# Layer 1's last six gate and up pairs by seven quarter products instead of eight, with B's plain blocks ahead of them and one set of down weights for both halves

## The chip, the cores and the metric

The kernel runs on one core of one Trainium2 chip. The metric is device time in microseconds (us); less is better. TensorE (PE in the profile) does the matmuls, VectorE (DVE), ScalarE (ACT) and GpSimd (POOL) do the rest, and SyncE (SP) and ScalarE issue most DMAs.

## The reference

Two layers over x of 1024 positions by 1024 features, fp32, each with a mixer and a SwiGLU feed-forward of 2816 hidden features. Layer 0's mixer is a gated MLP beside trailing means; layer 1's is RWKV-7, a recurrence over positions whose output `y * g` is multiplied by `w_o`.

```python
def swiglu(hn, w_gate, w_up, w_down):
    return (jax.nn.silu(hn @ w_gate) * (hn @ w_up)) @ w_down

for layer in range(DEPTH):
    hn = rms_norm(h, mix_norm[layer])
    h = h + mixer(hn)            # layer 0: gMLP and pooling; layer 1: RWKV-7, (y * g) @ w_o
    h = h + swiglu(rms_norm(h, ffn_norm[layer]), ffn_w_gate[layer], ffn_w_up[layer], ffn_w_down[layer])
return rms_norm(h, final_norm)
```

## The kernel before

**Tiling.** The positions are two halves, A and B, of 512 each (`HT`). Features stand on the partitions in eight chunks of 128, so a half of an activation is eight tiles of 128x512. The hidden features are 22 blocks of 128, in 11 pairs. A fp32 product is made of three matmuls on rounded parts: high by high, high weight by low activation, low weight by high activation (`mm3`, L408; `split`, L158, makes the parts: ScalarE copies the high part, VectorE subtracts it, L160, for the low one). One gate or up block for one half is therefore 8 chunks by 3 = 24 matmuls of 128x512; a down block for one half is 24 as well.

**Seven products.** In layer 0, pairs 4 to 10 (`PORDER`) are made by a scheme of the Strassen and Winograd kind. A unit is one pair's gate or up weights (1024 by 256) against both halves. Its four weight quarters and four activation quarters are combined by additions, and seven quarter products (`quarter`, L739, 12 matmuls each) give what eight would. `full_steps` (L790) does it: `weights` (L794) makes the weight sums on VectorE (L797 to L806) and splits them; the activation sums t1 to t4 were made earlier. `first_steps` (L759) makes half A's plain block of a unit from two quarter products, and can keep the first of them, p1, in DRAM (`p1_d`) for `full_steps`, which then does five (60 matmuls). Layer 1 is plain everywhere before the change: `ffn` (L947) goes through groups of blocks, gates, ups and then their down products, for one half at a time.

**Order of the weights.** `plan` is a list of all weight loads in the order of their use. `take` (L147) hands out the next entry, starts the loads of the following ones and their splitting; all loads are issued from ScalarE's queue (L123) into three slots named `raw`. Entries can be pieces of an activation too: `push_act(("y", 1), ...)` puts the four pieces of the recurrence's output y, which goes through DRAM (`y_d`), into the same plan and the same three slots.

**Layer 1's end, before.** `recur` (L1474) runs half B's recurrence while `drive` (L1042) feeds it dense work of half A: `dense_a`, `ffn` over `TAIL`. When the recurrence's output of the last step (`yp`, L1496) is there, `post` normalizes it per head (L1698 to L1723), TensorE transposes it (`sm<-ident,ysb`), VectorE gates it (`gch`, L1740) and SyncE stores it (L1743). Half A's remaining gate, up and down blocks go on meanwhile, and y's pieces are loaded and split between them. `out_b` then does `out_proj` (L1783) for half B, B's norm follows, half A ends with `final_down` (L1798, the last down products in transposed form with the final norm), and half B's whole feed-forward ends the kernel, with its own loads of all gate, up and down weights. `residual` (L506) adds a finished product to the stream on VectorE (L507). In the profile dense products are L409 to L411, quarter products L744 to L746, final ones L1810 to L1812.

Of the kernel before, what the change touches and what calls it, by code (L numbers as in the profile page):

```python
# [9 lines left out]
F32 = mybir.dt.float32  # L10
F32R = mybir.dt.float32r
AF = mybir.ActivationFunctionType
ALU = mybir.AluOpType
# [28 lines left out]
PORDER = (4, 5, 6, 7, 8, 9, 10)  # L42


@with_exitstack
def tile_trunk(
# [175 lines left out]

    def push_ffn_event(l, h, kind, f, lean=False):
# [71 lines left out]
    p1_d = dram.tile([P, 2 * PAIRS, HT], F32, name="p1_d")  # L295
# [59 lines left out]
    y1, o1, begun = push_act(("y", 1), y_d[1]), push_o(1), False  # L355
    TAIL = G1A[1] + G1A[2] + G1A[3]
    for e in ffn_events(TAIL, True):
        begun = begun or e == ("u", G1A[2][0][0])
        if e == ("u", G1A[3][0][0]):
            for go in o1:  # L360
                go()
        if e[0] != "d":
            push_ffn_event(1, 0, *e)
        if begun and e[0] in "gu":
            next(y1, None)
    push_ffn(1, 1)
# [387 lines left out]
    def save_hidden(fp, h, f, s):  # L754
        t = fp.tile([P, 2, HT], F32R, tag="hid", bufs=2, name="hid")
        split(s, t[:, 0, :], t[:, 1, :])
        sp.dma_start(hid_d[h][:, f], t.bitcast(F32))

    def first_steps(blocks, hn, fp):  # L759

        b11, b21 = (parts_of(hn, slice(k, k + 4)) for k in (0, 4))
        sg, prev = {}, []

        def second(i, f, n, w, o):
            quarter(o, parts_of(w, HI), b21, False)
            if n == 0:
                sg[f] = fp.tile([P, HT], F32, tag="t2", bufs=2, name="sg")
                act.activation(sg[f], o, AF.Silu)
            else:
                s = sg.pop(f)  # L770
                dve.tensor_tensor(out=s, in0=s, in1=o, op=ALU.mult)
                save_hidden(fp, 0, f, s)

        for i, f, n, kept in blocks:
            w = take(("first", f, n))
            o = mmt()
            quarter(o, parts_of(w, LO), b11, True)
            if kept:
                t = fp.tile([P, HT], F32, tag="t1", bufs=2, name="p1")
                act.activation(t, o, AF.Copy)  # L780
                sp.dma_start(p1_d[:, 2 * i + n, :], t)
            yield 0.5
            if prev:
                second(*prev.pop())
                yield 0.5
            prev.append((i, f, n, w, o))
        second(*prev.pop())
        yield 0.5

    def full_steps(blocks, kept, x, fp, wp):  # L790
# [3 lines left out]
        def weights(i):  # L794
# [12 lines left out]
            c = [wp.tile([P, D], F32R, tag=t, bufs=2, name=t) for t in ("chi", "clo")]  # L807
# [11 lines left out]
        makes["full0"], makes["full1"] = weights0, weights  # L819
# [5 lines left out]
        def finish(i, n, j, s, psum=None):  # L825
# [4 lines left out]
            else:  # L830
                dve.tensor_tensor(out=s, in0=gates.pop((i, j)), in1=s if psum is None else psum, op=ALU.mult)
                save_hidden(fp, j % 2, 2 * i + j // 2, s)

        for i, n in blocks:
            k = i in kept
            a = mmt()
            w = take(("full0", i, n))
# [10 lines left out]
            b, c, d = take(("full1", i, n))  # L848
# [98 lines left out]
    def ffn(l, h, hn, fp, groups=GROUPS, last=False, nd=3, after=None, between=iter(()), early=False, then={}):  # L947
# [3 lines left out]
        for kind, f in ffn_events(groups, early):  # L951
            if kind in "gu" and last and f in groups[-1] and len(turned) < 4 and (kind, f) != ("g", groups[-1][0]):
# [26 lines left out]
            else:  # L979
# [6 lines left out]
                for m in range(KT):  # L986
# [7 lines left out]
                    if m == KT - 1 and f[-1] in then:  # L994
                        then[f[-1]]()
# [36 lines left out]
    def exhaust(gen):  # L1032
        for _ in gen:
            pass
# [753 lines left out]
    def turn(h, j):  # L1788

        t = fin_pool.tile([P, D], F32, tag="turn", bufs=4, name="turn")  # L1790
# [284 lines left out]
    flag, hnB = [], []  # L2075

    def out_b():
        exhaust(out_proj(1, ys))
        hnB.extend(norm_split(1, C_FFN + 8, b))

    def y_pieces():
        while not flag:
            yield
        yield from take_act(("y", 1))

    dense_a = ffn(
        1, 0, hnA, f, TAIL, last=True, between=y_pieces(), early=True,
        then={G1A[1][-1][-1]: lambda: flag.append(1), G1A[2][0][-1]: out_b},
    )
    drive(until(dense_a, flag), recur(1, wp, in_pieces(hp, 0, h_d[0, 1]), RATIO), RATIO)  # L2090
    wp_es.close()
    ps_es.close()
    ps_es = open_psum("psd2", DENSE)
    b, b_es = open_pool(name="act3", bufs=1, side="left")
    hb_pool, hb_es = open_pool(name="hb2", bufs=1, side="left")
    fin_pool, fin_es = open_pool(name="fin", bufs=1, side="left")
    fgb = fin_pool.tile([P, D], F32, name="fgb")
    act.dma_start(fgb, final_norm.partition_broadcast(P))
    reload(hb_pool, 1, h_d[1, 1])
    ys = open_act(("y", 1), b)  # L2100
    drive(dense_a)
    drive(ffn(1, 1, hnB, f, last=True, early=True))
    for e in (fin_es, hb_es, b_es, hp_es, nxt["a_es"], f_es, ps_es):
        e.close()
# [30 lines left out]
```

## Time and profile before

| what | value |
|---|---|
| median of 3 runs (lowest, highest) | 2382.71 us (2379.66, 2390.3) |
| the profiled execution's own time | 2386.18 us |
| its span | 2384.4 us |
| mean granted TensorE clock | 0.987 |
| PE busy | 2315.2 us, 97% |
| DVE busy | 1465.3 us, 61% |
| ACT busy | 947.4 us, 40% |
| DMA | 347.97 MB, mean 146 GB/s |

The profile describes one execution. Its first part gives each engine's busy time and share, its second the span in 40 slices, its fourth the chain of work that ended last. A row of the timeline reads: start in us, duration, engine, line, operation, output<-inputs, and in brackets how long the engine had been idle and what it waited for. A row of the table of windows gives, for a stretch of time, each engine's busy time with the number of its instructions, then the granted TensorE clock, the DMA engines' busy share and GB/s.

### The profile page before, as it was taken

What the parts mean: (1) busy time and instruction counts of PE and PEld (TensorE: products, weight loads), DVE (VectorE), ACT (ScalarE), POOL (GpSimd) and SP (SyncE); (2) the same over time, 40 slices, a digit from 0 to 9 for tenths busy, and PEclk for the clock granted to TensorE, in tenths of its full rate; (3) what the DMA queues carried; (4) which work ended last, traced back from release to release, by engine and by line L of the source; (5) the groups of instructions that cost most, each with busy time, mean ns of one, the idle gap of its engine ahead of it and who ended that gap; (6) DMA issues with size and microseconds to landing.
All of it is one profiled execution on the core that took longest, in us unless ns stands there. A gap on an engine that the chain in (4) does not pass through costs nothing.

```text
span 2384.4 us, 37572 instructions
## 1 busy us (share of the span) xinstructions
PE 2315.2 (97%) x15315; PEld 1892.5 (79%) x15315; DVE 1465.3 (61%) x2312; ACT 947.4 (40%) x1467; POOL 182.5 (8%) x207
## 2 busy tenths in 40 slices
PE   8999999999999999999989899999999999999998
PEld 6888888888888888777767678787778788888886
DVE  6445775656567958757768858856664546443443
ACT  6233443444223765423336565433232225222223
POOL 0200000000000022101100122201010001000001
PEclk9999999999999999999989999999999999999999
DMA  5114473333765476776545475776525324333231
GB/s 182 53 45 143 150 193 97 107 111 128 290 234 193 144 191 157 220 220 171 145 138 139 143 197 148 210 221 181 158 85 162 116 80 133 115 97 97 83 112 45
DMA packets 422605, 347.97 MB, mean 146 GB/s; under 512 B 95200, under 2 KB 368736, under 8 KB 420128
## 3 DMA queue, kind: packets, MB, share of 16 engines
q10 hardware_dynamic: 266048, 195.33, 27.7%
q1 hardware_dynamic: 155168, 146.05, 20.0%
q0 software_dynamic: 1216, 4.20, 0.8%
q8 instruction: 120, 1.97, 0.4%
q14 instruction: 53, 0.43, 0.1%
HBM read 266.47 MB, written 79.04 MB: 145 GB/s over the span
## 4 chain that ended last, share of the span: by engine, by line
PE 83%; DVE 7%; DMA 4%; ACT 2%; issue 2%; POOL 1%; SPq 0%; ACTq 0%; POOLq 0%; DVEq 0%
PE mm L409 19%; PE mm L411 19%; PE mm L410 19%; PE mm L744 5%; PE mm L746 5%; PE mm L745 5%; PE sm L1496 4%; DVE wlo L160 1%; DMA raw<-y_d 1%; DVE it L1448 1%; PE yp L1496 1%; PE aux L1420 1%; PE aux L1421 1%; PE mm L594 1%; PE aux L1422 1%
## 5 line engine op out<-in xcount | busy, mean ns | idle before, releaser
L409 PE MATMUL mm<-ahi,whi 128*128 128x512 f32 x1376 | 542.5, 397 | 12.8 <-ACT ahi L159 11.9
L411 PE MATMUL mm<-ahi,wlo 128*128 128x512 f32 x1376 | 542.1, 394 | 3.7 <-DVE wlo L160 3.7
L410 PE MATMUL mm<-alo,whi 128*128 128x512 f32 x1376 | 542.6, 394 | 2.3 <-DVE alo L160 2.3
L159 ACT ACTIVATE whi<-raw 128x1024 fp32r<-128x1024 f32 (+2 forms) x284 | 286.4, 1014 | 522.6 <-PE mm L410 410.6
L160 DVE TENSOR_TENSOR wlo<-raw,whi 128x1024 fp32r<-128x1024 f32 (+2 forms) x284 | 340.4, 1202 | 223.6 <-ACT whi L159 206.1
L409 PEld LDWEIGHTS mm<-ahi,whi 128*128 128x128 f32 x1376 | 260.0, 189 | 71.6 <-ACT ahi L159 13.2
L411 PEld LDWEIGHTS mm<-ahi,wlo 128*128 128x128 f32 x1376 | 260.0, 189 | 60.6 <-DVE wlo L160 4.6
L410 PEld LDWEIGHTS mm<-alo,whi 128*128 128x128 f32 x1376 | 260.2, 189 | 59.8 <-DVE alo L160 4.0
L507 DVE TENSOR_TENSOR h<-h,mm 128x512 f32<-128x512 f32 x276 | 186.3, 685 | 161.7 <-PE mm L411 157.2
L969 DVE TENSOR_TENSOR sg<-sg,mm 128x512 f32<-128x512 f32 x52 | 35.7, 687 | 138.3 <-PE mm L411 138.3
L409 PE MATMUL mm<-hidhi,wdhi 128*128 128x512 f32 x304 | 117.9, 394 | 1.9 <-ACT sg L961 1.9
L410 PE MATMUL mm<-hidlo,wdhi 128*128 128x512 f32 x304 | 119.6, 394 | 0.0
L411 PE MATMUL mm<-hidhi,wdlo 128*128 128x512 f32 x304 | 119.5, 393 | 0.0
L744 PE MATMUL mm<-ahi,whi 128*128 128x512 f32 x296 | 115.7, 391 | 0.0
L745 PE MATMUL mm<-alo,whi 128*128 128x512 f32 x296 | 115.3, 390 | 0.0
L746 PE MATMUL mm<-ahi,wlo 128*128 128x512 f32 x296 | 113.7, 390 | 0.0
L159 ACT ACTIVATE wdhi<-raw 128x1024 fp32r<-128x1024 f32 x42 | 43.4, 1057 | 161.9 <-PE mm L410 117.8
L409 PEld LDWEIGHTS mm<-hidhi,wdhi 128*128 128x128 f32 x304 | 57.5, 189 | 14.6 <-ACT sg L961 2.3
L160 DVE TENSOR_TENSOR wdlo<-raw,wdhi 128x1024 fp32r<-128x1024 f32 x42 | 51.4, 1224 | 27.7 <-ACT wdhi L159 27.7
L411 PEld LDWEIGHTS mm<-hidhi,wdlo 128*128 128x128 f32 x304 | 57.5, 189 | 12.3 <-issue 0.5
L410 PEld LDWEIGHTS mm<-hidlo,wdhi 128*128 128x128 f32 x304 | 57.4, 189 | 11.9
L744 PEld LDWEIGHTS mm<-ahi,whi 128*128 128x128 f32 x296 | 55.6, 188 | 11.7 <-issue 0.2
(394 smaller groups left out, 4232.9 us busy)
## 6 DMA issues: line engine op xcount, KB each, us to landing
raw<-in_ffn_w_down_dram ACTq DMA_DIRECT2D x88, 512.0 KB
raw<-in_ffn_w_gate_dram ACTq DMA_DIRECT2D x74, 512.0 KB
raw<-in_ffn_w_up_dram ACTq DMA_DIRECT2D x74, 512.0 KB
hid_d<-hid SPq DMA_DIRECT2D x36, 512.0 KB
ar<-ab_d SPq DMA_DIRECT2D x16, 1024.0 KB
hd<-hid_d SPq DMA_DIRECT2D x26, 512.0 KB
raw<-in_ab_w_in_dram ACTq DMA_DIRECT2D x16, 512.0 KB
raw<-in_ab_w_out_dram ACTq DMA_DIRECT2D x16, 512.0 KB
```

The costliest lines, as they stand in the source:

```text
L159: act.activation(hi, src, AF.Copy)
L160: (eng or dve).tensor_tensor(out=lo, in0=src, in1=hi.bitcast(F32), op=ALU.subtract)
L409: pe.matmul(o, whi, xhi, start=first, stop=False)
L410: pe.matmul(o, whi, xlo, start=False, stop=False)
L411: newest[0] = pe.matmul(o, wlo, xhi, start=False, stop=last).ins
L507: dve.tensor_tensor(out=H[h][:, m, :], in0=H[h][:, m, :], in1=o, op=ALU.add)
L594: pe.matmul(ops[j], xhi[:, k, sl], whi[:, kk], start=(k == 0), stop=False)
L744: pe.matmul(o, wh[:, k, :], x[0][:, k, :], start=st, stop=False, skip_group_check=True)
L745: pe.matmul(o, wh[:, k, :], x[1][:, k, :], start=False, stop=False, skip_group_check=True)
L746: pe.matmul(o, wl[:, k, :], x[0][:, k, :], start=False, stop=k == 3, skip_group_check=True)
L969: dve.tensor_tensor(out=s, in0=s, in1=o, op=ALU.mult)
L1496: i = f(*args, **kw)
```

## The change

Pairs 5 to 10 of layer 1 (`LATER`), 12 units, are made by seven products. The new order is:

- `dense_a` beside the recurrence covers only blocks 2 to 9 of half A with their downs, and its `then` hook, now called ahead of the last down group, makes the first two units' plain block of half A (`first_steps` with `keep`, key `first1`, p1 and hidden rows to DRAM). H[0] is stored to `hs_d`.
- After the recurrence come four more such units, between them the loads of y's four pieces; then `out_proj` for B, then the last six units, beside which B's norm is made (`norm_b`).
- `plain_b` makes B's blocks 0 to 9 plainly (480 matmuls); beside it `combine1` makes the activation sums t1 to t4 from rows that it loads from `nb_d` and `n_d[1]`.
- `full_steps` over the 12 units, five quarter products each (720 matmuls). The tile `c` (the split of two weight sums) uses the buffers of `b12` (`pair_of`).
- `last_downs`: for blocks 10 to 19 both halves with one set of weights, then blocks 0 to 9 for B, then blocks 20 and 21 by `final_down`, A then B. Hidden rows come from `hid1_d`.

```diff
+LATER = (5, 6, 7, 8, 9, 10)
+AHEAD_IN = 2
...
-    TAIL = G1A[1] + G1A[2] + G1A[3]
+    UNITS = mats(LATER)
+    TAIL = groups_to(2, 2 * LATER[0])
+    GD = [[2 * i, 2 * i + 1] for i in LATER[:-1] + tuple(range(LATER[0])) + LATER[-1:]]
...
     for e in ffn_events(TAIL, True):
+        if e == ("d", TAIL[-1]):
+            push_units(UNITS[:AHEAD_IN])
...
-    push_ffn(1, 1)
+    y1 = push_act(("y", 1), y_d[1])
+    push_units(UNITS[AHEAD_IN : AHEAD_IN + 3])
+    for unit in (UNITS[AHEAD_IN + 3], None, None):
+        next(y1)
+        if unit:
+            push_units([unit])
+    next(y1)
+    for go in push_o(1):
+        go()
+    push_units(UNITS[AHEAD_IN + 4 :])
...
-    drive(until(dense_a, flag), recur(1, wp, in_pieces(hp, 0, h_d[0, 1]), RATIO), RATIO)
+    drive(dense_a, recur(1, wp, in_pieces(hp, 0, h_d[0, 1]), RATIO), RATIO)
...
+    reload(hb_pool, 1, h_d[1, 1])
+    ys = open_act(("y", 1), xa)
+    got_y = take_act(("y", 1))
...
+    exhaust(first_steps(all_units[AHEAD_IN : AHEAD_IN + 4], hnA, f, "first1", hid1_d, between=y_calls()))
+    exhaust(got_y)
...
+    exhaust(out_proj(1, ys, after_b))
...
+    drive(first_steps(all_units[AHEAD_IN + 4 :], hnA, f, "first1", hid1_d), norm_b(norm_bcast(acc[0])), 2.0)
...
+    drive(plain_b(), combine1(), 1.0)
...
+    cs = [b.tile([P, 4, HT], F32R, tag="b12" + t, name="c" + t) for t in ("hi", "lo")]
...
+    steps = full_steps(UNITS, LATER, x, f, wp, "Full", hid1_d, pair_of)
...
-    drive(ffn(1, 1, hnB, f, last=True, early=True))
+    exhaust(last_downs())
```

**What moves.** Everything up to the middle of half B's recurrence stands as before, with line numbers 33 to 46 higher. The next rows are TensorE's at the recurrence's end; `sm<-ident,ysb` are the eight transposes of y, `hidhi` and `wdlo` belong to half A's down products, `ahi` and `whi` to gate and up products. Before:

```order
L411 MATMUL mm<-ahi,wlo 128x512
L409 MATMUL mm<-ahi,whi 128x512
L1496 MATMUL sm<-ident,ysb 128x128 x7
L410 MATMUL mm<-alo,whi 128x512
L411 MATMUL mm<-ahi,wlo 128x512
```

And in the change:

```order
L444 MATMUL mm<-hidhi,wdlo 128x512
L1540 MATMUL sm<-ident,ysb 128x128 x8
L777 MATMUL mm<-ahi,whi 128x512
L778 MATMUL mm<-alo,whi 128x512
L779 MATMUL mm<-ahi,wlo 128x512
```

Before, 78 matmuls of 128x512 stand between the last `yp` product and the seven transposes (68 ahead of the first of the eight); now 30, all of them down products. Behind the transposes stand 34 quarter-product matmuls of units 2 to 4, then second quarters of these.

The next rows are ScalarE's queue at the same place; `raw<-y_d` is the load of a piece of y into a weight slot, `ahi` its split, `sg`, `t` and `hidhi` belong to blocks of half A. Before:

```order
L159 ACTIVATE wdhi<-raw 128x1024
L123 DMA raw<-y_d_83 128x1024
L159 ACTIVATE ahi<-raw 128x1024
L159 ACTIVATE whi<-raw 128x1024
L972 ACTIVATE hidhi<-sg 128x512
L123 DMA raw<-in_ffn_w_down_dram 128x1024
```

And in the change, from the recurrence's last copy on:

```order
L1690 ACTIVATE ysb<-yp 128x512
L1759 ACTIVATE ysb<-ysb,mean,var 128x64 x8
L125 DMA raw<-y_d_82 128x1024
L125 DMA raw<-in_ffn_w_up_dram 128x8x128
L125 DMA raw<-y_d_82 128x1024
L822 ACTIVATE t_16825<-mm 128x512
L161 ACTIVATE ahi<-raw 128x1024
L822 ACTIVATE t_16847<-mm 128x512
L125 DMA raw<-y_d_82 128x1024
L161 ACTIVATE ahi<-raw 128x1024 x2
L125 DMA raw<-y_d_82 128x1024
L161 ACTIVATE whi<-raw 128x1024
```

Before, weight loads, splits and hidden rows of half A stood between y's pieces. Now the first piece's load follows the last `ysb` work directly, and the next weights (`whi`) and the copies of p1 (`t`) stand behind it.

SyncE's queue there, where `y_d<-gch` is y's store, `p_d` the store of a p1, `hid_d_89` hidden rows of the new scheme, `hs_d_91` half A's stream and `h<-h_d` the 2 MB reload of half B's stream. Before:

```order
L1743 DMA y_d_83<-gch 1024x1x128
L1684 DMA gch<-g_d_1981 128x8x128
L1743 DMA y_d_83<-gch 1024x1x128
L1845 DMA h<-h_d_87 128x4096
```

And in the change:

```order
L1728 DMA gch<-g_d_1986 128x8x128
L812 DMA hid_d_89<-hidhi 128x512
L812 DMA hid_d_89<-hidlo 128x512
L2121 DMA hs_d_91<-h 128x512 x7
L1889 DMA h<-h_d_86 128x4096
L2121 DMA hs_d_91<-h 128x512
L1787 DMA y_d_82<-gch 1024x1x128
L823 DMA p_d<-t_16825 128x512
```

The last store of y stood ahead of the reload of half B's stream and now stands behind it and behind the stores of half A's stream.

More of the change, by code (lines that the diff above doesn't have):

```diff
@@ L771, in second @@
                 dve.tensor_tensor(out=s, in0=s, in1=o, op=ALU.mult)
-                save_hidden(fp, 0, f, s)
+                if lean:
+                    ts = [fp.tile([P, HT], F32R, tag=t, bufs=3, name=t) for t in ("hidhi", "hidlo")]
+                    split(s, *ts)
+                    for j in range(2):
+                        sp.dma_start(to[0][:, f, j], ts[j].bitcast(F32))
+                else:
+                    save_hidden(fp, 0, f, s, to)
         for i, f, n, kept in blocks:
-            w = take(("first", f, n))
+            w = take((key, f if key == "first" else i, n))
             o = mmt()
@@ L785, in first_steps @@
                 yield 0.5
+            next(between, None)
             prev.append((i, f, n, w, o))
@@ L2074, in tile_trunk @@
     hnA = nxt["hn"]
[L2075 to L2084, printed above, removed]
+    all_units = [(i, 2 * i, n, True) for i, n in UNITS]
     dense_a = ffn(
-        1, 0, hnA, f, TAIL, last=True, between=y_pieces(), early=True,
-        then={G1A[1][-1][-1]: lambda: flag.append(1), G1A[2][0][-1]: out_b},
-    )
-    drive(until(dense_a, flag), recur(1, wp, in_pieces(hp, 0, h_d[0, 1]), RATIO), RATIO)
@@ new lines, in tile_trunk, with after_b, norm_b @@
+    exhaust(got_y)
+    acc, add = running_sums(1)
+    def after_b(m):
+        sp.dma_start(hs_d[1][:, m, :], H[1][:, m, :])
+        add(m)
+    exhaust(out_proj(1, ys, after_b))
+    x = {n: [b.tile([P, 4, HT], F32R, tag=n + t, name=n + t) for t in ("hi", "lo")] for n in ("b12", "b22")}
+    def norm_b(bc_):
+        for m in range(KT):
+            t = nt.tile([P, HT], F32, tag="nsq", bufs=2, name="hn")
+            dve.scalar_tensor_tensor(
+                out=t, in0=H[1][:, m, :], scalar=col(C_FFN + 8 + m), in1=bc_, op0=ALU.mult, op1=ALU.mult
+            )
+            split(t, *(y[:, m % 4, :] for y in x["b12" if m < 4 else "b22"]))
+            sp.dma_start(nb_d[:, m, :], t)
+            yield 1.0
@@ new lines, in plain_b @@
+    def plain_b():
+        for fd in range(2 * LATER[0]):
+            for kind in "gu":
+                w = take((kind, 1, 1, fd))
+                o = mmt()
+                quarter(o, parts_of(w, LO), x["b12"], True)
+                yield 0.5
+                quarter(o, parts_of(w, HI), x["b22"], False)
+                if kind == "g":
+                    s = f.tile([P, HT], F32, tag="t2", bufs=2, name="sg")
+                    act.activation(s, o, AF.Silu)
+                else:
+                    dve.tensor_tensor(out=s, in0=s, in1=o, op=ALU.mult)
+                    save_hidden(f, 1, fd, s, hid1_d)
+                yield 0.5
@@ new lines, in last_downs @@
+    def last_downs():
+        turned, wd = {0: [], 1: []}, {}
+        for gi, g in enumerate(GD):
+            for fd in g:
+                wd[fd] = take(("D", fd))
+            if gi + 1 < len(GD):
+                load_hid(gi + 1, hslot)
+            if gi + 1 == len(GD):
+                break
+            for h in halves_of(gi):
+                for m in range(KT):
+                    o = mmt()
+                    ms = slice(m * P, (m + 1) * P)
+                    for i, fd in enumerate(g):
+                        hd = held[h, fd]
+                        mm3(o, wd[fd][0][:, ms], wd[fd][1][:, ms], hd[:, 0, :], hd[:, 1, :], i == 0, i == 1)
+                    residual(m, h, o)
+                    if gi == len(GD) - 2 and m % 2:
+                        turned[0].append(turn(0, m // 2))
+        for h in range(2):
+            hid = {fd: (held[h, fd][:, 0, :], held[h, fd][:, 1, :]) for fd in g}
+            if h == 0:
+                turned[1].extend(turn(1, j) for j in range(4))
+            yield from final_down(h, g, wd, hid, turned[h])
```

142 lines of the change are left out of this document (114 added, 28 removed).

## The prediction

> **What bounds the kernel now.** I read the page first: which engine fills the span, and the chain that ended last.
>
> ```profile
> PE 2315.2 (97%) x15315; PEld 1892.5 (79%) x15315; DVE 1465.3 (61%) x2312; ACT 947.4 (40%) x1467; POOL 182.5 (8%) x207
> ```
>
> ```profile
> PE 83%; DVE 7%; DMA 4%; ACT 2%; issue 2%; POOL 1%; SPq 0%; ACTq 0%; POOLq 0%; DVEq 0%
> ```
>
> TensorE is busy 97% and 83% of the chain. Matmuls left out are worth their full time only where nothing else becomes late, so I read the stages next, in the table of windows.
>
> ```profile
> 200.00:600.00 400.00, 400.00 (x1770) 330.84 (x1769) 253.59 (x366) 165.92 (x257) 2.56 (x3) 1.00 0.44 134
> 600.00:700.00 100.00, 99.09 (x435) 81.16 (x435) 57.38 (x75) 22.63 (x25) 5.11 (x5) 1.00 0.72 257
> 1230.00:1265.00 35.00, 22.12 (x72) 16.81 (x71) 26.60 (x42) 16.33 (x24) 1.20 (x2) 0.71 0.81 241
> 1800.00:1900.00 100.00, 98.15 (x432) 80.73 (x431) 45.80 (x53) 26.83 (x32) 0.00 (x0) 1.00 0.41 124
> 2100.00:2300.00 200.00, 200.00 (x884) 165.71 (x883) 83.49 (x95) 50.93 (x62) 0.00 (x0) 1.00 0.32 97
> ```
>
> 200 to 600 is layer 0's own stage of seven products, 600 to 700 its down products from stored hidden rows, 1230 to 1265 the place where half A's y of layer 1 comes back from DRAM, 1800 on the stage that the change rewrites. There TensorE has almost nothing to gain in waits; the waits from 1600 on say the same:
>
> ```profile
> PE sm L1496 <- DVE gt L1537: 4.5, 3, 2.8
> PE mm L409 <- ACT sg L961: 1.9, 1, 1.9
> ```
>
> The 4.5 us lie inside the recurrence, which stays. The 1.9 us are the one wait of the dense stage (98.15 of 100 between 1800 and 1900); its code goes.
>
> **Fewer products.** A unit plainly costs 2 blocks x 2 halves x 24 = 96 matmuls; by seven products 84. Twelve units: 144 fewer. At full rate 400 us / 1770 = 0.226 us each, so 144 x 0.226 = **-32.5 us**, all of it on the path, and -1.9 us with the wait above.
>
> **The turn of y: the dearest term.** Rows of the recurrence's end, in the timeline:
>
> ```profile
> 1768.80 0.92 PE L1496 MATMUL yp<-uv,gt 128*64 128x64 f32 x24
> ...
> 1782.42 0.68 DVE L1723 TENSOR_TENSOR ysb<-ysb,vch 128x512 f32<-128x512 f32 x1
> ...
> 1787.63 0.93 PE L1496 MATMUL sm<-ident,ysb 128*128 128x128 f32 x7
> 1788.16 2.16 DVE L1740 SCALAR_TENSOR_TENSOR gch<-sm,vec,gch 128x128 f32<-128x128 f32 x8 [0.29 <-PE sm L1496]
> ```
>
> Call the end of the last yp product, 1769.7, T0. y is ready for the transposes at 1783.1, T0+13.4, by VectorE's and ScalarE's normalization. Before, 68 matmuls (15.4 us) covered that; now 30 (6.8 us). VectorE has about two fewer residual additions between (of the size of the 0.68 us row, 0.5 to 0.7 each, so about -1.0), so TensorE idles from about +6.8 to +12.4: **5.6 us**. What comes then is seen once already, in layer 0's end, where half A's y goes through DRAM with little to cover it:
>
> ```profile
> 1231.76 0.54 SPq L1743 DMA_DIRECT2D y_d<-gch  x1
> 1235.35 1.49 ACTq L123 DMA_DIRECT2D raw<-y_d  x3
> 1240.70 2.23 ACT L159 ACTIVATE ahi<-raw 128x1024 fp32r<-128x1024 f32 x2 [2.67 <-DMA raw<-y_d]
> ...
> 1241.81 0.79 PE L409 MATMUL mm<-ahi,whi 128*128 128x512 f32 x1 [8.89 <-ACT ahi L159]
> ...
> 1244.22 2.61 ACTq L123 DMA_DIRECT2D raw<-in_rwkv_w_o_dram  x4
> ...
> 1244.54 0.63 PE L411 MATMUL mm<-ahi,wlo 128*128 128x512 f32 x1
> ...
> 1248.38 0.63 PE L411 MATMUL mm<-ahi,wlo 128*128 128x512 f32 x1
> ...
> 1250.05 1.06 ACT L159 ACTIVATE whi<-raw 128x1024 fp32r<-128x1024 f32 x1 [1.81 <-DMA raw<-in_rwkv_w_o_dram]
> ```
>
> From store to load 3.59 us, from load to split 5.35, from a w_o load to its split 5.83. After the idle 8.89 us the matmuls between 1244.54 and 1248.38 start (1248.38 - 1244.54) / 9 = 0.427 us apart instead of 0.226, nearly half speed, and ten of them lose 2.0 us. The window's 72 records, of 155 that fit 35 us at full rate, say that this place loses up to 18.7 us in all.
>
> The Trainium skill, "TensorE: Matmul & The Clock Gate", Part 1, speaks against new gaps: a gate passes half of the clock's pulses after an idle window of about 3.4 us and opens after about as long busy. The trace agrees on the factor (0.427 to 0.226). As an estimate from the page a gap costs 3.4 x 1/2 = 1.7 us, and the sum below, with two long gaps, would be 2 x 0.3 = 0.6 us lower by it.
>
> The walk with these durations: transposes 1.2 and gch 2.2 us bring the store to +16, the first load of y to +19.5, its split to +25. TensorE meanwhile has 34 matmuls from +13.6, ten at half clock: 7.7 + 2.0, to +23.3. Then come second quarters, which need copies of p1 that stand behind y's load in ScalarE's queue: the first is there at +21, the second stands behind the split of the first piece, +26: **1 us**. At +29.3 the next unit's weights are wanted (`whi` at the end of the ScalarE rows). Their split stands behind that of the third piece of y, whose slot comes free with the low part of the first (+27.3), lands +5.35 later and is split in 1.1: +33.7, so **4.4 us**. `out_proj`'s first weights wait for a slot in the same ring and 5.83 us more: about **2.7 us**, and the second quarter beside it **1.4** for its copy of p1 (both estimates of the same walk). With half clock after the two longest gaps, 2.0 each: 5.6 + 2.0 + 1 + 4.4 + 2.0 + 2.7 + 1.4 = **+19 us**. Bounds: 8 us (the transposes and their half clock alone; the rest hidden by the matmuls behind) and 25 us (5.6 and the 18.7 that layer 0's place loses). I take 19, near layer 0's figure, since the queue is the same. SyncE's queue is the reason why the store could be later still: the 2 MB reload and eight stores of half A's stream stand ahead. An issue takes about 0.5 us, as the store's own row has it, and doesn't wait for its landing; they go out while y is still normalized, so nothing is added.
>
> **B's norm.** Its chain in layer 0 runs from the sums to the first product:
>
> ```profile
> 1244.14 0.16 DVE L454 TENSOR_SCALAR nrs<-aux 128x4 f32<-128x4 f32 x1
> ...
> 1251.37 0.75 DVE L1111 SCALAR_TENSOR_TENSOR hn<-h,vec,aux 128x512 f32<-128x512 f32 x1 [1.88 <-PE aux L461]
> ```
>
> 7.2 us and eight scaled rows behind it. Six units, 144 matmuls or 32.5 us, cover that; without them it would cost 7 to 15. I take +0.5 (0 to 3). `combine1` puts 16 subtractions and 16 low parts beside 480 matmuls: nothing (cover 108 us against some 22 of VectorE).
>
> **The stage of five products.** 12 units of 60 matmuls, 13.55 us each. VectorE has 17 operations of 128x512 per unit (four sums, five low parts of weights, three copies with p1, two additions, 1.5 gating products and 1.5 low parts of hidden rows). In layer 0:
>
> ```profile
> 345.00:600.00 255.00, 255.00 (x1126) 211.25 (x1126) 152.68 (x227) 107.25 (x176) 0.00 (x0) 1.00 0.35 117
> ```
>
> ```profile
> DVE s3lo L160 <- ACT s3hi L159: 22.3, 12, 5.3
> DVE hid L160 <- ACT hid L159: 11.2, 17, 0.7
> DVE wlo L160 <- ACT whi L159: 10.0, 9, 3.1
> DVE s L797 <- DMA raw<-in_ffn_w_up_dram: 6.1, 7, 1.2
> ```
>
> ```profile
> L160 DVE TENSOR_TENSOR wlo<-raw,whi 128x512 fp32r<-128x512 f32 x28 | 18.9, 687 | 2.3 <-ACT whi L159 1.7
> L159 ACT ACTIVATE whi<-raw 128x512 fp32r<-128x512 f32 x28 | 16.8, 628 | 6.4 <-PE mm L745 3.9 <-DVE raw L800 1.7 <-PE mm L746 0.8
> ```
>
> A unit there takes 84 x 0.226 = 19.0 us of TensorE (so 13.4 units in 255 us) and 152.68 / 13.4 = 11.4 us of VectorE, with TensorE never waiting. Now it is 17 x 0.687 = 11.7 against 13.55, or 86%: it fits, but closely. `s3hi` has a single buffer, so ScalarE splits (0.628) only after TensorE's last use in the unit before, and TensorE then wants it: some 0.7 us in every second unit, **+4 us** (0 to 12). At the stage's start the tile `c` must wait for the last use of `b12` before the second raw slot empties and the next load comes: **+1.7** (0 to 4; a load and its split are 5.4 to 5.8 us, of which a product or two hide most).
>
> **The last downs.** For B's groups alone two blocks' weights and hidden rows, 2 MB, go with 48 matmuls, 10.8 us: 194 GB/s. The row 600 to 700 has 257 GB/s with TensorE at 99.09%. About 1% of 100 us: **+1** (0 to 4), the order of the two final parts included. The new 136 issues on SyncE wait for nothing that TensorE needs but the ones above.
>
> **The sum.** 2386.2 - 32.5 - 1.9 + 19 + 0.5 + 4 + 1.7 + 1 = 2378.0 against the profiled execution's 2386.18. That lies 3.5 above the median of the runs, so in terms of the median **2374.5**. A measurement of this kernel tells about 0.5% (12 us: below 2370.8, above 2394.6) from no change.
>
> **Rivals.**
> 1. *y is covered after all.* The 24 second-quarter matmuls and the products of units 4 and 5 hide the loads, and only the transposes' wait and its half clock remain (8 us instead of 19), and `s3hi` never makes TensorE wait (0 instead of 4), as in layer 0, whose row 200 to 600 has no wait with the same single buffer. For it: before, y went through DRAM beside dense work and cost 1.9 us. Against: three raw slots for y, w_o and weights together. Time: 2374.5 - 11 - 4 = 2359.5. Faster.
> 2. *VectorE becomes the bound of the five-product stage.* If the waits for ScalarE and loads in layer 0's rows are not slack but stay with each unit, they add (22.3 + 11.2 + 10.0 + 6.1) / 13.4 = 3.7 us to 11.7: 15.4 us a unit against 13.55, so 12 x 1.85 = 22 us in place of 4. Time 2374.5 + 18 = 2392.5; with the turn at its upper bound (+6) 2398.5. It decides from 13.55 us a unit on. Against: `s3lo`'s wait is longest 5.3 us, which looks like VectorE running ahead of TensorE. Centre 2396, slower.
> 3. *The saving isn't there:* matmuls were not the limit. The rows at 400.00 of 400 and 200.00 of 200 exclude it; under 0.02.
>
> **How the numbers follow.** The forecast with its own range of 2365 to 2384 has 0.46, rival 1 0.32, rival 2 0.17, the rest 0.05. Faster by over 0.5% needs under 2370.8: rival 1 nearly whole (0.30) and a quarter of the forecast's case (0.11): 0.41. Slower, above 2394.6: most of rival 2 and some of the rest, 0.14. Within: 0.45. The range takes rival 1 with its good half, down to 2352, and rival 2 up to 2397.
>
> **What would show it.** In the profile after: 144 fewer 128x512 matmuls; TensorE idle before the transposes of y by 5 to 6 us and half clock behind; a wait on `whi` of 4 us some 20 us later, none if rival 1 holds; waits on `s3hi` in the five-product stage, with VectorE under 90% there; over 95% and TensorE waiting for VectorE's `wlo` or `clo` in every unit is rival 2. A wait on the raw loads of hidden rows in the last 110 us would be a term I left out, and a recurrence that itself runs longer would make the reading of the order wrong.

## The result and the profile after

| | before | changed |
|---|---|---|
| median of 7 runs each | 2386.00 us (2379.66 to 2395.07) | 2368.74 us (2367.38 to 2372.49) |
| ratio, 95% interval | | 0.9924 [0.9908, 0.994] |
| profiled execution, its span | 2386.18, 2384.4 us | 2372.49, 2370.8 us |

The change is faster by 0.76%, 17 to 18 us. The forecast was 8 us less than the kernel before (2374.5 against the 2382.71 of three runs; those three lay low). The direction held, and the gain is twice what was forecast as likeliest. The measured time lies in the range, 2352 to 2397, but that range is wide enough to hold a gain of 31 us and a loss of 14.

The windows of the kernel after, with the same columns as those of before:

```profile
200.00:600.00 400.00, 400.00 (x1770) 330.74 (x1770) 252.87 (x365) 166.03 (x258) 2.56 (x3) 1.00 0.44 134
...
1760.00:1850.00 90.00, 80.60 (x423) 65.05 (x418) 44.70 (x72) 28.81 (x42) 2.90 (x1) 0.94 0.64 200
...
2040.00:2203.00 163.00, 159.42 (x697) 130.33 (x697) 119.02 (x183) 49.27 (x77) 0.00 (x0) 1.00 0.55 188
2260.00:2360.00 100.00, 100.00 (x474) 82.89 (x472) 61.50 (x89) 30.86 (x58) 10.82 (x12) 1.00 0.33 116
```

1760 to 1850 is the turn of y, with 9.4 us of TensorE idle; the five-product stage lasts from 2003 to 2168, so 2040 to 2203 holds most of it and 35 us of down products. VectorE is at 73% there, and also in the stage alone (119.5 of 164 us), not at the 86% of the prediction: 189 operations stand in those 164 us instead of 204, in part because the first two units' weight sums are made earlier; and operations of 687 ns start as little as 600 ns apart, so their busy times overlap. The downs from 2260 on have no wait. TensorE's waits from 1600 us on:

```profile
PE sm L1540 <- DVE ysb L1767: 6.2, 4, 3.7
PE mm L777 <- ACT whi L161: 5.2, 2, 4.2
PE mm L777 <- ACT s3hi L161: 3.0, 6, 0.5
PE sm L1540 <- DVE gt L1581: 1.9, 2, 1.1
PE mm L777 <- DVE t L905: 1.1, 1, 1.1
```

**The turn of y went mostly as walked.** From its timelines (T0, the end of the last yp product, is 1765.7 here):

```profile
1764.53 1.15 PE L1540 MATMUL yp<-uv,gt 128*64 128x64 f32 x32
...
1776.44 0.45 PE L1540 MATMUL sm<-ident,ysb 128*128 128x128 f32 x1 [3.74 <-DVE ysb L1767]
1777.97 1.73 PE L1540 MATMUL sm<-ident,ysb 128*128 128x128 f32 x7 [1.08 <-DVE ysb L1767]
...
1781.07 0.54 SPq L1787 DMA_DIRECT2D y_d<-gch  x1
...
1785.98 0.34 ACTq L125 DMA_DIRECT2D raw<-y_d  x1
...
1798.97 0.50 PE L777 MATMUL mm<-ahi,whi 128*128 128x512 f32 x1 [4.19 <-ACT whi L161]
```

TensorE idles 4.8 us before the transposes, in two parts (3.74 and 1.08; 5.6 forecast), the store goes out at T0+15.4 (+16), the first load of y at +20.3 (+19.5), and TensorE waits 4.2 us for the weights behind y's third piece (4.4), up to +33.3 (+33.7). `out_proj`'s first weights and the copy of p1 beside them cost nothing (2.7 and 1.4 forecast). Behind both gaps the clock is half:

```profile
1778.00:1782.00 4.00, 4.00 (x13) 3.47 (x14) 2.16 (x8) 0.00 (x0) 0.00 (x0) 0.50 0.63 260
1782.00:1786.00 4.00, 4.00 (x17) 3.27 (x16) 0.00 (x0) 0.00 (x0) 0.00 (x0) 0.91 0.47 135
...
1799.00:1803.00 4.00, 3.76 (x9) 2.75 (x10) 1.97 (x3) 1.91 (x4) 0.00 (x0) 0.60 0.58 205
```

About seven matmuls start 0.427 us apart behind each gap, so a gap costs 1.4 to 1.6 us there, not 2.0: the 1.7 us estimated from the Trainium skill, "TensorE: Matmul & The Clock Gate", Part 1, was the nearer one.

**Where the rest came from.** The start varies from execution to execution. y is transposed in sets of eight, one set for each chunk of 128 positions. The third set from the end ends a stretch of the same code in all kernels here, and in the fourteen profiles it starts between 1695.8 and 1702.0: at 1695.96 before and at 1699.89 after. Counted from them, the two profiles differ by (2384.4 - 1695.96) - (2370.8 - 1699.89) = 688.4 - 670.9 = 17.5 us, as the runs do. It divides at the last yp product:

- **Behind it 614.7 us before, 605.1 after.** At 0.2257 us each the 2612 and 2478 matmuls take 589.5 and 559.3, so 25.2 and 45.8 us are something else: +20.6 us, where the prediction had 19 + 0.5 + 4 + 1.7 + 1 - 1.9 = +24.3.
- **Ahead of it 73.8 us before, 65.8 after.** Ten matmuls (2.3 us) moved behind it. The other 5.7 us are nowhere in the prediction.

The timelines show a place for the 5.7 us. Before:

```profile
1714.45 1.06 ACT L159 ACTIVATE wdhi<-raw 128x1024 fp32r<-128x1024 f32 x1 [4.37 <-DMA raw<-in_ffn_w_down_dram]
...
1715.54 1.23 DVE L160 TENSOR_TENSOR wdlo<-raw,wdhi 128x1024 fp32r<-128x1024 f32 x1 [3.90 <-ACT wdhi L159]
1716.68 1.28 DVE L1537 TENSOR_TENSOR gt<-sm,gm 128x512 f32<-128x512 f32 x2
...
1717.42 1.98 PE L1496 MATMUL sm<-ar 64*64 64x128 f32 x30 [2.77 <-DVE gt L1537]
```

And in the change at the same step of the recurrence:

```profile
1717.52 1.29 DVE L1581 TENSOR_TENSOR gt<-sm,gm 128x512 f32<-128x512 f32 x2 [2.08 <-PE sm L1540]
```

Before, VectorE stood at the low part of block 10's down weight, for whose load ScalarE had waited 4.37 us, with the recurrence's gt behind it; TensorE idled 2.77 us, and half clock followed, here in the windows before (the change's clock is 1.00 there):

```profile
1719.00:1723.00 4.00, 4.00 (x71) 3.56 (x66) 2.67 (x4) 0.00 (x0) 0.00 (x0) 0.50 0.95 250
```

In the change the last group of half A's blocks there is 8 and 9, there is no third down weight at that place, and gt waits for TensorE instead.

### The profile page after: what moved, and what is told of

It is laid out like the page before. It is cut to its first block, busy times and chain, and to the rows that moved or that the text cites. A ratio compares the mean times of both kernels' runs of the same rounds, so it can differ in the third digit from the quotient of the medians.

```text
span 2370.8 us, 37920 instructions
## 1 busy us (share of the span) xinstructions
PE 2283.6 (96%) x15171; PEld 1861.3 (79%) x15171; DVE 1552.3 (65%) x2496; ACT 952.7 (40%) x1507; POOL 181.8 (8%) x207
## 5 line engine op out<-in xcount | busy, mean ns | idle before, releaser
L162 DVE TENSOR_TENSOR wlo<-raw,whi 128x1024 fp32r<-128x1024 f32 (+2 forms) x274 | 314.1, 1151 | 164.8 <-ACT whi L161 135.8
L443 PE MATMUL mm<-alo,whi 128*128 128x512 f32 x864 | 342.2, 396 | 2.4 <-DVE alo L162 2.1
L442 PE MATMUL mm<-ahi,whi 128*128 128x512 f32 x832 | 329.4, 399 | 13.1 <-ACT ahi L161 11.5
L444 PE MATMUL mm<-ahi,wlo 128*128 128x512 f32 x832 | 328.7, 395 | 2.9 <-DVE wlo L162 2.9
L777 PE MATMUL mm<-ahi,whi 128*128 128x512 f32 x488 | 193.0, 396 | 5.6 <-ACT whi L161 5.2
L442 PEld LDWEIGHTS mm<-ahi,whi 128*128 128x128 f32 x832 | 157.1, 189 | 50.7 <-ACT ahi L161 12.8
L778 PE MATMUL mm<-alo,whi 128*128 128x512 f32 x488 | 191.1, 392 | 0.0
L779 PE MATMUL mm<-ahi,wlo 128*128 128x512 f32 x488 | 188.7, 391 | 0.0
L442 PE MATMUL mm<-hd,dhi 128*128 128x512 f32 x368 | 144.4, 392 | 1.1 <-DVE h L540 1.1
L444 PE MATMUL mm<-hd,dlo 128*128 128x512 f32 x368 | 143.4, 390 | 0.0
L443 PE MATMUL mm<-hd,dhi 128*128 128x512 f32 x368 | 143.2, 389 | 0.0
L777 PEld LDWEIGHTS mm<-ahi,whi 128*128 128x128 f32 x488 | 92.4, 189 | 26.8 <-ACT whi L161 6.1
L161 ACT ACTIVATE dhi<-raw 128x1024 fp32r<-128x1024 f32 x40 | 40.5, 1052 | 171.7 <-PE mm L443 135.6
L779 PEld LDWEIGHTS mm<-ahi,wlo 128*128 128x128 f32 x488 | 92.3, 189 | 19.5
L442 PEld LDWEIGHTS mm<-hd,dhi 128*128 128x128 f32 x368 | 69.1, 188 | 16.3 <-DVE h L540 1.9
L444 PEld LDWEIGHTS mm<-hd,dlo 128*128 128x128 f32 x368 | 69.1, 188 | 14.5
L443 PEld LDWEIGHTS mm<-hd,dhi 128*128 128x128 f32 x368 | 69.1, 188 | 14.4 <-issue 0.2
```

The lines of the kernel that those rows point to most:

```text
L161: act.activation(hi, src, AF.Copy)
L162: (eng or dve).tensor_tensor(out=lo, in0=src, in1=hi.bitcast(F32), op=ALU.subtract)
L442: pe.matmul(o, whi, xhi, start=first, stop=False)
L443: pe.matmul(o, whi, xlo, start=False, stop=False)
L444: newest[0] = pe.matmul(o, wlo, xhi, start=False, stop=last).ins
L777: pe.matmul(o, wh[:, k, :], x[0][:, k, :], start=st, stop=False, skip_group_check=True)
```

## The experiments

Each kernel was timed beside the kernel before, and the ratio is to that. "From the transposes" is the span counted from the third-last set of transposes, as above: 688.4 us before, 670.9 in the change. One such number comes from one execution, and a part of it is chance: right behind that set the clock was 0.50 for 3.4 us in six of the fourteen profiles, those of the kernel before and of the change among them, and full in eight. Among kernels with the same code up to the last yp product, those with half clock there needed 1.6 us more to that product (68.5 against 66.9 with AHEAD_IN = 4; 65.7 and 65.8 against 64.1 and 64.2 in the change and experiments 6, 7 and 9). The experiments were timed in four sessions on three chips, so their ratios are compared through the kernel before.

**1. Block 10's low part on GpSimd** (on the kernel before).

```diff
+        if key == ("d", 1, 0, 10):
+            split(view(raw), view(hi), view(lo), pool)
+            ready[i] = hi, lo
+            return
         splits.get(key[0], lambda i, *t: split(*t))(key[1], view(raw), view(hi), view(lo))
```

> The kernel before, with one thing changed: the low part of half A's down weight for block 10 is subtracted on GpSimd instead of VectorE, where it stood right ahead of the recurrence's gt products. Theory 1 (in the kernel before that subtraction waited for a weight load and held gt back, so TensorE idled 2.8 us and then ran at half clock; the change only happened to move it away, which gave it some 5.5 us that the prediction did not have): TensorE's wait for gt after 1600 us falls from 4.5 us (longest 2.8) to under 2.5 (longest about 1.1), and the kernel is 4 to 6 us faster than before. Rival (the changed kernel's shorter recurrence was that one execution's chance, or comes from the dense work moved out of it): time within 1.5 us of before, and another wait takes the place.

Ratio 0.9993 [0.998, 1.0006]; 73.8 us up to the last yp product, as before. The theory fell in this form. TensorE's waits from 1500 us on, the two longest, and the rows of GpSimd and ScalarE behind the first:

```profile
PE sm L1500 <- ACT uv L1622: 4.0, 2, 3.6
PE sm L1500 <- DVE gt L1541: 3.0, 3, 2.1
```

```profile
1721.50 2.34 POOL L164 TENSOR_TENSOR wdlo<-raw,wdhi 128x1024 fp32r<-128x1024 f32 x1 [9.88 <-PE sm L1500]
```

```profile
1720.37 1.06 ACT L163 ACTIVATE wdhi<-raw 128x1024 fp32r<-128x1024 f32 x1 [4.46 <-DMA raw<-in_ffn_w_down_dram]
1723.87 0.37 ACTq L123 DMA_DIRECT2D raw<-in_ffn_w_gate_dram  x1
1724.37 0.59 ACT L1622 ACTIVATE uv<-sm 64x512 f32<-64x512 f32 x1 [2.94 <-POOL wdlo L164]
```

The wait only moved, to ScalarE. The weight's split ends there at 1721.43. The load of the next gate weight stands behind it and waits until GpSimd, with 2.34 us for what took VectorE 1.23, has read the slot; the recurrence's uv copy stands behind that load. The edit made this wait itself, so it leaves open what freeing VectorE alone is worth. (The next expectation puts it down to the split.)

**2. Block 10's down weight one step later** (on the kernel before; for half B's block 10 as well, since both use the list).

```diff
-                if early:
+                if early and f != 10:
                     yield "t", f
             if gi + 1 < len(groups):
                 yield "g", groups[gi + 1][0]
+            if early and 10 in g:
+                yield "t", 10
```

> The kernel before, with one thing changed: half A's down weight for block 10 is taken one step later, behind the gate of block 11. Moving only its subtraction off VectorE changed nothing, since ScalarE then held the recurrence's uv copy back behind the same weight's split (3.6 us). Theory 1, mended (the load of that weight is late, and everything of the recurrence that stands behind its split on ScalarE and VectorE waits; the change has no down weight at that place): the stretch from the transposes of the chunk before to the last yp product, 73.8 us before and 65.8 in the change, falls to 66 to 70 us, and the kernel is 4 to 7 us faster than before. Rival (the stretch is shorter in the change because less dense work and fewer residual additions stand in it): it stays at 72 to 74 us, time within 1.5 us of before.

The stretch up to the last yp product falls from 73.8 to 67.3 us, as the mended theory has it (eight matmuls, 1.8 us, moved behind it; gt's longest wait is 1.2). From the transposes it is 683.7, 4.7 less than before. Of these some 1.6 are the chance named above, since the clock behind the transposes is 0.50 in the profile before and 1.00 here, so about 3 are left to the edit. The runs don't show a gain: ratio 0.9997 [0.9982, 1.0012], at most 4.3 us, which doesn't exclude 3. So the profiles show that the blocked queues lengthen the stretch (experiment 11 brings them back); how much they are worth in the median of the runs stays open.

**3. Four units ahead of the last down group instead of two** (on the change).

```diff
-AHEAD_IN = 2
+AHEAD_IN = 4
```

> The changed kernel with AHEAD_IN = 4: four units' first products instead of two among the dense work beside the recurrence, so 68 matmuls instead of 30 stand between the last yp product and the transposes of y, and 4 units instead of 6 beside B's norm. Theory 1 (TensorE idles 4.8 us before the transposes and loses about 2 us at half clock behind that because 30 matmuls do not cover the normalization of y): that wait is gone, 5 to 7 us faster than the changed kernel, about 2362 us. Rival (y's chain ends when it ends, and the cover taken from behind the transposes or from the norm is missing there): the 4.2 us wait for whi grows or TensorE waits for B's norm, and the time moves by less than 2 us.

Ratio 0.9895 [0.9877, 0.9913], 2365.2 us where the kernel before took 2389.14: 24 us against the change's 18. From the transposes 665.6, 5.4 less than the change. The wait before the transposes is gone, as theory 1 has it, and so is the one for whi at the turn. A new one stands behind the transposes: TensorE's waits from 1765 to 1850:

```profile
PE mm L777 <- ACT t L822: 5.2, 2, 4.3
PE mm L444 <- DVE wlo L162: 0.8, 1, 0.8
PE mm L442 <- ACT whi L161: 0.4, 1, 0.4
```

Its queues say why. SyncE's and ScalarE's rows:

```profile
1783.34 0.32 SPq L1889 DMA_DIRECT2D h<-h_d  x1
1783.75 0.86 SPq L2121 DMA_DIRECT2D hs_d<-h  x2
1786.36 0.54 SPq L1787 DMA_DIRECT2D y_d<-gch  x1
```

```profile
1795.99 0.34 ACTq L125 DMA_DIRECT2D raw<-y_d  x1
```

Here 9.6 us lie between y's store and its first load, where the change has 4.9 and half A's y, at the end of layer 0's work, had 3.6. The 2 MB reload goes out 3 us ahead of the store; experiment 10 moves it away.

**4. Two more units ahead of y's first load** (on the change; four beside the norm).

```diff
-    push_units(UNITS[AHEAD_IN : AHEAD_IN + 3])
-    for unit in (UNITS[AHEAD_IN + 3], None, None):
+    push_units(UNITS[AHEAD_IN : AHEAD_IN + 5])
+    for unit in (UNITS[AHEAD_IN + 5], None, None):
...
-            if call > 4:
+            if call > 8:
...
-    exhaust(first_steps(all_units[AHEAD_IN : AHEAD_IN + 4], hnA, f, "first1", hid1_d, between=y_calls()))
+    exhaust(first_steps(all_units[AHEAD_IN : AHEAD_IN + 6], hnA, f, "first1", hid1_d, between=y_calls()))
...
```

> The changed kernel with two of the six units beside B's norm moved in front of the first load of y: six units instead of four between the recurrence and out_proj, y's pieces behind the fifth of them. Theory 1 (the 4.2 us wait for the weights behind y's pieces in ScalarE's queue and the raw slots is a lack of cover between the store and the load of y): the wait on whi falls from 5.2 us to under 1, the half clock behind it goes, and the idle before the transposes stays; 4 to 7 us faster than the changed kernel, about 2363 us. Rival (the queue itself is the limit: whatever stands behind y's pieces waits for the ring of three slots): a wait of 3 to 5 us stays at the last unit or at the first product of out_proj, time within 2 us.

Ratio 0.9914 [0.9896, 0.9932]; from the transposes 666.4, 4.5 less than the change. The waits for whi fall from 5.2 to 0.8 us (the 4.2 at the turn is gone), a wait of 2.0 for a copy of p1 takes part of their place, and the transposes wait 1.1 longer, with 24 matmuls ahead of them instead of 30. Theory 1 holds in the profile; the ratio's interval takes in the change's ratio, so the runs don't show a gain.

**5. Both** (experiments 3 and 4 together, two units beside the norm).

> The changed kernel with both moves: AHEAD_IN = 4 and two more units ahead of y's first load, so that only two units, 48 matmuls or 10.8 us, are left beside B's norm. Theory 1 (each gap is a lack of cover at its place, and the norm needs 7 us for its sum and some 6 for the rows that plain_b needs first): neither the transposes nor the weights behind y wait, 4 us less than with AHEAD_IN = 4 alone, but 2 to 4 us of wait for the norm come back; the sum is 0 to 2 us faster than AHEAD_IN = 4 alone. Rival (the norm's chain is covered by far less): no wait at the norm, 4 to 5 us faster than AHEAD_IN = 4 alone.

Ratio 0.9947 [0.9928, 0.9966], and 676.0 from the transposes: slower than either. TensorE's waits from 1640 on, among them:

```profile
PE mm L777 <- ACT b12hi L161: 6.5, 2, 5.0
PE mm L777 <- ACT whi L161: 4.4, 2, 3.9
...
PE mm L778 <- DVE b12lo L162: 1.4, 1, 1.4
```

Now the norm's rows (`b12hi`, `b12lo`) are late by 6.5 us and 1.4 more for their low parts: more than the 2 to 4 of theory 1, and far from the rival. And 3.9 us of wait for the weights behind y stay, where theory 1 had none. 48 matmuls don't cover B's norm; 96 do (experiments 3 and 4 have no such wait).

**6. Two buffers for the split third weight sum** (on the change).

```diff
-            d = [wp.tile([P, HT], F32R, tag=t, bufs=1, name=t) for t in ("s3hi", "s3lo")]
+            d = [wp.tile([P, HT], F32R, tag=t, bufs=2 if pair_of else 1, name=t) for t in ("s3hi", "s3lo")]
```

> The changed kernel with two buffers instead of one for the split third weight sum (s3hi, s3lo) in layer 1's five-product stage. Theory 1 (in every second unit TensorE waits 0.5 us until ScalarE has split s3 into the buffer just released, and some more in refilling): the 3.0 us of waits on s3hi are gone and the stage is 3 to 6 us shorter, about 2364 us. Rival (TensorE only waits there because VectorE and the loads of p1 are late, and it will wait for them instead): another wait of the same size in the stage, time within 1.5 us.

Ratio 1.0003 [0.9986, 1.002]: the whole gain of the change is gone. From the transposes 689.8, 18.9 more than the change. TensorE's waits from 1500 on, their first row:

```profile
PE mm L777 <- DVE t L905: 19.7, 11, 3.5
```

The waits on s3hi are gone, and eleven on VectorE's L905 stand there: the sum that reads the accumulator before TensorE may add to it again. The single buffer had set VectorE's order. With two, the program puts the next unit's weight sums (L841, L843) and a hidden row ahead of L905:

```profile
2065.41 0.69 DVE L841 TENSOR_TENSOR s<-raw 128x512 f32<-128x512 f32 x1 [0.67 <-DMA raw<-in_ffn_w_gate_dram]
...
2066.14 0.69 DVE L843 TENSOR_TENSOR raw<-raw 128x512 f32<-128x512 f32 x1
...
2067.43 0.69 DVE L162 TENSOR_TENSOR hid<-t,hid 128x512 fp32r<-128x512 f32 x1 [0.60 <-ACT hid L161]
2068.04 0.68 DVE L905 TENSOR_TENSOR t<-t,mm 128x512 f32<-128x512 f32 x1
...
2068.77 0.50 PE L777 MATMUL mm<-ahi,s3hi 128*128 128x512 f32 x1 [2.42 <-DVE t L905]
```

The sums wait for a load, the hidden row for ScalarE, and what TensorE needs waits behind them. This is the place and the size of rival 2 (22 us), but not by VectorE's throughput: it does the same operations.

**7. Two more subtractions per unit on VectorE** (on the change, to a tile that nobody reads).

```diff
+            if pair_of:
+                for _ in range(2):
+                    spare = wp.tile([P, HT], F32, tag="spare", bufs=1, name="spare")
+                    dve.tensor_tensor(out=spare, in0=a22, in1=a22, op=sub)
```

> The changed kernel with two subtractions of 128x512 added on VectorE per unit in the five-product stage, written to a tile that nobody reads. With 17 operations VectorE is busy 11.7 us of the 13.55 us of a unit, with 19 it is 13.1. Theory 1 (it is VectorE's throughput that decides, from 13.55 us on): TensorE's waits in the stage grow by under 4 us in all. Rival (VectorE's order decides: any operation that stands ahead of the sum which TensorE waits for adds to the wait, as with two buffers for s3, where nothing was added and the stage took 19 us more): 8 us or more are lost, as waits of TensorE on VectorE's t or wlo.

In the stage TensorE waits 2.5 us for s3hi (3.0 in the change), 2.1 for t (1.1) and 2.1 for whi (1.0); behind the last yp product 606.2 us against 605.1. The waits grow by 1.6 us in all, as theory 1 has it. The ratio, 0.9948 [0.993, 0.9965], overlaps the change's and can't tell a loss of up to 11 us from none, so only the profile of one execution speaks against the rival.

**8. y's pieces loaded from SyncE's queue** (with AHEAD_IN = 4).

```diff
-            act.dma_start(dst(raw), src)
+            (sp if plan[i][0][0] == ("y", 1) else act).dma_start(dst(raw), src)
```

> The changed kernel with AHEAD_IN = 4 and with y's pieces loaded from SyncE's queue instead of ScalarE's. Theory 1 (behind the transposes TensorE waits because ScalarE, in order, stands at the load of y until y is stored, and the copies of p1 queue behind it: 4.3 us on that copy with AHEAD_IN = 4): the wait on the copy (L822) falls from 5.2 us to under 1.5, and the kernel is 3 to 6 us faster than with AHEAD_IN = 4 alone; what is left is the wait for y and for the first weights of out_proj. Rival (the copies are free, but the next thing in the queue, the split of a piece of y that has not landed, holds them just as long): a wait of 3 to 4 us for ScalarE stays, time within 1.5 us of AHEAD_IN = 4 alone.

Ratio 0.9922 [0.9902, 0.9943]. TensorE waits 6.2 us for the copy, not less: it stands behind the split of y's first piece in ScalarE's queue, and the piece lands no sooner (its split starts at 1801.76, with AHEAD_IN = 4 alone at 1800.21). Behind the last yp product it is 598.3 us against 598.7. The rival holds in the profile; the ratio is higher, with an interval that overlaps that of experiment 3.

**9 and 10. The reload of half B's stream behind y's first piece** (on the change, and with AHEAD_IN = 4).

```diff
-    reload(hb_pool, 1, h_d[1, 1])
...
+            if call == 5:
+                H[1] = hb_pool.tile([P, KT, HT], F32, tag="h", name="h")
+                dve.tensor_copy(H[1][:, 0, 0:1], ys[0][:, 0, 0:1].bitcast(F32))
+                sp.dma_start(H[1], h_d[1, 1])
```

> The changed kernel with the 2 MB reload of half B's stream made to wait for y's first piece, so that it no longer goes out ahead of y's last store on SyncE's queue. In the changed kernel 4.9 us lie between that store's issue and the first load of y, 3.6 in layer 0's place of the same kind, 9.6 with AHEAD_IN = 4, where the reload goes out 2.8 us ahead of the store instead of 8.6. Theory 1 (a store lands later by what stands ahead of it on its queue, contrary to the prediction, which counted only the issue): 4.9 falls to 3.5 to 4.0, the wait for whi behind it from 4.2 to about 3, 1 to 2 us faster than the changed kernel. Rival (the load's issue is late for another reason: ScalarE or the slot): it stays at 4.9, time within 1 us.

> The same with AHEAD_IN = 4. Theory 1: the 9.6 us between the store of y and its first load fall to 4 to 6 (five to seven stores of half A's stream still stand ahead), the wait for the copy of p1 behind it (5.2 us) to under 1.5, and the kernel is 3 to 6 us faster than with AHEAD_IN = 4 alone, some 2361 us where the kernel before takes 2386. Rival: the stores of half A's stream are what holds y's store; 9.6 stays above 8, time within 1.5 us of AHEAD_IN = 4 alone.

With AHEAD_IN = 4 the 9.6 us fall to 3.5, so there the reload was what held y's store. In the change itself the distance stays at 5.0, as the rival has it: what makes 4.9 of 3.6 there is not the reload, and stays open. And both kernels lose by the edit in the profile: behind the last yp product 611.3 us against 605.1, and 601.4 against 598.7. Their ratios are 0.9946 [0.9928, 0.9963] and 0.9922 [0.9904, 0.9939], above those without the edit, with intervals that overlap. The reload now runs beside y's later pieces. The split of y's third piece in the change:

```profile
1796.92 1.06 ACT L161 ACTIVATE ahi<-raw 128x1024 fp32r<-128x1024 f32 x1 [2.30 <-DMA raw<-y_d]
```

The same split, and TensorE's wait behind it, in the first of the two:

```profile
1797.03 1.06 ACT L161 ACTIVATE ahi<-raw 128x1024 fp32r<-128x1024 f32 x1 [6.55 <-DMA raw<-y_d]
```

```profile
1799.09 0.80 PE L777 MATMUL mm<-ahi,whi 128*128 128x512 f32 x1 [8.53 <-ACT whi L161]
```

ScalarE waits 6.55 us for the third piece instead of 2.30, and TensorE's wait for whi doubles from 4.2 to 8.5. Neither theory had this: the cost moved from the store to the loads.

**11. Five pairs by seven products instead of six** (on the change).

```diff
-LATER = (5, 6, 7, 8, 9, 10)
+LATER = (6, 7, 8, 9, 10)
```

> The changed kernel with five pairs instead of six by seven products (LATER = 6 to 10). 24 matmuls come back, 5.4 us; two more plain blocks of half A stand in the dense work beside the recurrence, so that 82 matmuls instead of 30 lie ahead of the transposes of y, y's store goes out ahead of the reload, and four units instead of six stand beside B's norm. Theory 1 (each product left out is worth its full time, but the gaps at y's turn, some 4.8 + 4.2 us of waits and 4 at half clock, are a lack of cover): the gaps shrink by 9 to 12 us, the sixth pair also cost 0.7 us at s3hi, so 4 to 7 us faster than the changed kernel. Rival (the gaps come back at another place, as with two more units ahead of y): slower by up to 5.4 us.

Ratio 0.993 [0.9913, 0.9948], from the transposes 670.7: the same as with six, so the 4 to 7 us didn't come. Behind the last yp product it went as theory 1 has it: TensorE's waits at the turn fall from 9.4 to 3.6 us, and what is not matmul time from there to the end (602.5 less 2508 x 0.2257) is 36.4 us against 45.8, 9.4 less, for 5.4 us of products. But ahead of it the stretch is 68.2 us with six matmuls fewer, 3.8 more than in the change. With this grouping of half A's blocks a down weight's low part stands ahead of gt again, and TensorE's gap is back:

```profile
1721.79 1.98 PE L1540 MATMUL sm<-ar 64*64 64x128 f32 x30 [2.58 <-DVE gt L1581]
```

That is experiment 2 the other way round, in the changed kernel: 5.4 - 9.4 + 3.8 = -0.2 us.

**12. The copies of p1 on VectorE** (with AHEAD_IN = 4).

```diff
-                act.activation(t, o, AF.Copy)
+                dve.tensor_copy(t, o)
```

> The changed kernel with AHEAD_IN = 4 and with the copies of p1 out of PSUM made on VectorE instead of ScalarE, where they stand behind the load and the split of y's first piece. Theory 1 (ScalarE's order alone makes TensorE wait there: 5.2 us on L822 with AHEAD_IN = 4): that wait goes and 3 to 5 us are gained on AHEAD_IN = 4 alone. Rival (y's own chain, from its store through the three raw slots to out_proj's weights, is the limit behind it): the wait on the copies goes, and a wait of 3 to 5 us for whi, of the last unit or of out_proj, takes its place; time within 1.5 us of AHEAD_IN = 4 alone.

Ratio 0.9912 [0.9895, 0.9928]. From the last yp product to the end 598.4 us, with ScalarE's copies 598.7. The waits from 1765 to 1850:

```profile
PE mm L777 <- ACT whi L161: 2.4, 1, 2.4
PE mm L442 <- ACT whi L161: 1.9, 1, 1.9
PE mm L777 <- DVE t L822: 0.8, 1, 0.8
```

5.2 us on the copy became 0.8 on the copy and 2.4 + 1.9 on weights behind y in the ring. The rival holds: with AHEAD_IN = 4 y's own way through DRAM, the three slots and `out_proj`'s weights is what ends last.

The lowest ratio is that of experiment 3, the change with AHEAD_IN = 4: 0.9895 [0.9877, 0.9913]. Its interval overlaps those of the change and of experiments 4 and 12, so a gain on these is seen in the profile (6.4 us less behind the last yp product than in the change), not shown by the runs.

## Why the prediction was right or wrong

1. **Fewer products, -32.5 us: right.** The records have 15315 - 15171 = 144 matmuls fewer, and the downs run at full rate with no wait.
2. **"The 4.5 us lie inside the recurrence, which stays": this step failed.** The wait for gt fell from 4.5 to 1.9 us, and the stretch up to the last yp product is 5.7 us shorter than its ten moved matmuls explain. I took the recurrence's code for its queues. The dense work that the change alters stands in the same queues; experiments 2 and 11 show, in one profile each, that a down weight there holds the recurrence back. Taking it away gave about 3 us, bringing it back cost 3.8; the rest of the 5.7 has no test. It is the largest part of the error in the profile; its worth in the runs' median was not resolved.
3. **The turn of y, +19: right up to the second gap, too dear behind it.** Two gaps (4.8, 4.2) stand against 5.6 and 4.4, half clock of about 1.5 each against 2.0, and 0.4 for the copies of p1 against 1. `out_proj` and the copy beside it waited for nothing, where 2.7 + 1.4 were forecast. That is some 12.5 us. From T0 to the first product on s3hi, 2008.9, lie 243.2 us; its 991 matmuls take 223.7 and the transposes 1.2. The 18 left are these 12.5, 1.0 at the next stage's start, and some 5 of small instructions and slow restarts that had no term. So the sum of 19 + 0.5 + 1.7 is near 18 in part by luck.
4. **B's norm, +0.5: right** (no wait). Of the 144 matmuls of cover 96 are enough; with 48 the waits are 8 us.
5. **"An issue ... doesn't wait for its landing ..., so nothing is added": wrong when the reload stands close ahead.** With the 2 MB reload 3 us ahead of it, y's store to its load took 9.6 us, and 3.5 without (experiments 3 and 10). In the change, with 8.6 us between, it took 4.9 instead of 3.6; experiment 9 clears the reload of that. By the trace's semaphore records fifteen of the store's sixteen parts had landed 3.4 us after its issue and the last one 4.9 us after it; why that one was late stays open.
6. **The five-product stage, +4 and +1.7: right in place, a little low in all.** TensorE waited 3.0 us on s3hi in six places, 1.0 at the stage's start, and 1.1 on L905 near its end (2150.4), which had no term. From the first to the last product on s3hi lie 149.9 us for 634 matmuls, 143.1 us: 6.8 too long, the slow starts behind the waits included.
7. **Rival 1** did not occur: y was not covered (9.4 us of waits at the turn), s3hi made TensorE wait, and the time is 9 us above its 2359.5. It named the right direction, but the gain came from elsewhere. **Rival 2** did not occur; experiment 6 shows how near it was, by the order and not by the busy share.
8. **The centre.** It was put 3.5 us under the profile's sum because three runs had a median of 2382.71; over seven runs the kernel before has 2386.00, about the profiled execution's own time. Without that shift it would have been 2378.0, 9 us above the measured 2368.74 instead of 6: this part of the agreement is luck.

## What to carry to other kernels

A wait inside a stage that an edit "doesn't touch" can still go or come, if the edited work shares its in-order queues: read what stands ahead of the waiting instruction on the releasing engine before calling a wait fixed. A gap behind a round trip through DRAM is filled only while the cover lasts on both sides; moved work opened a gap at the next place in experiments 3, 5, 9, 10 and 12. A single buffer can be what keeps a good order: adding one cost 19 us here with no operation added.

## What the runs showed of the hardware

With a 2 MB load issued 3.0 us ahead of it on the same queue, a store's first dependent load went out 9.6 us after the store; with that load moved behind the store, 3.5 us after it (experiments 3 and 10). Where the 2 MB load went out beside a 512 KB load on another queue, the small one's data was split 8.7 us after its issue instead of 4.7 (experiment 9 and the change).

Gaps of 4.8 and 4.2 us left TensorE at a granted clock of 0.50 for about 3 us of matmuls each, and a gap of 2.8 us, in the recurrence before, did so for 4 us and more; the prediction had counted half clock behind its two longest gaps alone. The length of a gap does not decide it: behind the same gap of 1.23 us, ahead of the third-last transposes, the clock fell to 0.50 in six of the fourteen profiles and stayed at 1.00 in eight.
